# Two heads at once: scores as 64-row matmuls in an attention encoder on one Trainium2 core

## The chip, the cores and the metric

The kernel runs on one core of one Trainium2 chip. The metric is device time in microseconds (us) of one execution; lower is better. The core's engines work side by side and wait for one another through semaphores: TensorE (PE in the profile; PEld is its loading of stationary operands), VectorE (DVE), ScalarE (ACT), GpSimd (POOL) and SyncE (SP), which here only starts DMA transfers.

## What is computed

The reference is a two-layer encoder over 1024 tokens of width 1024, all in float32. Layer 0 uses mixer A (a neighbourhood attention), layer 1 uses mixer B (grouped-query attention). After each mixer come an output projection, a residual add and a gated per-layer embedding. The change touches mixer B, 16 query heads of width 64 that share 4 key/value heads:

```python
def mixer_b(h, w_in, q_norm_g, k_norm_g, w_out):
    proj = h @ w_in
    q, k, v, gate = jnp.split(proj, [MIX_WIDTH, MIX_WIDTH + kv_w, MIX_WIDTH + 2 * kv_w], axis=-1)
    q = rms_norm(q.reshape(b, s, B_Q_HEADS, HEAD_DIM), q_norm_g).transpose(0, 2, 1, 3)
    k = rms_norm(k.reshape(b, s, B_KV_HEADS, HEAD_DIM), k_norm_g).transpose(0, 2, 1, 3)
    ...
    q, k = _apply_axial_rope(q, tabs), _apply_axial_rope(k, tabs)
    ...
    sc = jnp.einsum('bkgqd,bksd->bkgqs', qb, k).astype(jnp.float32) * scale
    pr = jax.nn.softmax(sc, axis=-1).astype(v.dtype)
    o = jnp.einsum('bkgqs,bksd->bkgqd', pr, v)
    ...
    return (o * jax.nn.silu(gate)) @ w_out
```

## The kernel before, in words

**Number format.** TensorE takes fp32r operands, so a float32 value is held as a high part and a low part (names ending in h and l, or `KA` and `KB` for keys). A projection of two such operands is three matmuls: high by high, high by low, low by high (`split3`, all through the helper `mm`, line 300). That line therefore carries nearly all matmuls; they are told apart by the tiles they write: `d` a projection, `s` scores, `o` an attention output. `t` is written by transposes, which are TensorE instructions with a line of their own.

**Layout.** The normalised residual stream stands transposed in `HTh`/`HTl` and serves every projection. Weights come by DMA into `wstage` and are split into `wh`/`wl` by one ACT and one DVE instruction each (lines 215 and 216); a queue `WQ` brings them on in the order of use.

**One attention step of mixer B** covers one head and one tile of 128 queries, so there are 128 steps; they are listed with the two heads of a pair one after the other. A step has four parts:

- `f_S`: four matmuls write the scores of 128 queries by 1024 keys into `s` (two PSUM banks; there are two such buffers). The stationary tile `QS` has the head's query high part in the 64 partitions of one half and its low part in the other half; `KA` and `KB` hold the keys' high and low parts in both halves, so a matmul over 128 rows sums two products. Then DVE takes the row minimum `mn` (line 1047; the scores carry a minus sign).
- `f_E`: ACT computes the exponentials `P` and their row sums (line 1053).
- `f_T`: `P` is transposed in two blocks of four 128x128 transposes, each into a PSUM buffer `t` (two buffers). ACT writes the high part `PTh` (line 1065) and DVE the low part `PTl` (line 1066) out of each; after both the buffer is free.
- `f_AV`: on every second step, 16 matmuls multiply `V` by the `PTh` and `PTl` of two steps into `o`.

`q_stack` makes `QS`: four transposes of the rotated queries, a copy to `raw` on ACT, and for each head of the pair a cast of 64 rows on ACT (line 1029) and a subtraction on DVE (line 1030), the latter put off by two ticks. `head_end` takes a finished head out of `o` (an ACT copy, line 477, and a DVE sum, line 441, both on 64 rows), inverts the row sums and arranges gate, scaling and storing of a pair.

**What sets the order.** Each engine runs its instructions in the order in which the program lists them; nothing reorders them later. `mixer_b` lists 32 attention steps for each of four groups of heads, and `mix` lays the projection pieces of the group ("dense": gates, the next group's q, keys and values, and in the last group the products `pp`) between the parts of the steps, in the proportion of the weights that stand beside each part (`CB`, `CN`). After each part `pulse` moves the weight queue on by one and counts down work put off with `post.add(ticks, ...)`; `later` counts by steps. The order within the steps is

```python
att.append((later.tick, w[0]))
if av:
    att.append((lambda n=n: f_AV(*steps[n - 1]), w[1]))
te = [(lambda n=n: f_T(*steps[n]), w[2])]
if n + 1 < len(steps):
    te.append((lambda n=n: f_E(*steps[n + 1]), w[3]))
...
if n + 2 < len(steps):
    att.append((lambda n=n: f_S(*steps[n + 2]), w[4]))
```

so the scores run two steps ahead of the transposes and the exponentials one step. Before the groups a prologue projects the first keys, values and queries.

Of the kernel before, what the change touches and what calls it, by code (L numbers as in the profile page):

```python
# [21 lines left out]
NT = 8  # L22
# [8 lines left out]
CB = (1.25, 1.0, 2.0, 0.5, 1.0)  # L31
CN = (1.5, 0.0, 1.0, 1.0, 1.5)
# [5 lines left out]
FIN = (4, 4)  # L38
HOLD = 2
DP = 1  # L40
KD, KS = 3, 4
QD = (2, 5, 8)
QS_AT = 3
AGE, LAG = 3, 3
YS = (11, 11)
YLOAD_A, YLOAD_B = 1, 118
# [106 lines left out]
def trunk(ctx, tc, x, wts, rpb, gains, hgains, mask, rope, out):  # L153
# [275 lines left out]
    def head_end(sb, h, hf, rs, Ops, ylive, layer, gg, talloc):  # L429
        pair = h // 2  # L430
        b = (h % 2) * 64
        if h % 2 == 0:
            Y = sb.tile([128, 512], F32, name="Y", bufs=2)
            rb = sb.tile([128, 512], F32, name="rb", bufs=2)
            r8 = sb.tile([128, 8], F32, name="r8", bufs=4)
            ylive[pair, hf] = (Y, rb, r8, {})
        Y, rb, r8, tail = ylive[pair, hf]
        yh = Y[b:b + 64]

        def join():  # L440
            dve.scalar_tensor_tensor(yh, Ops[0:64], 0.5, yh, op0=ALU.mult, op1=ALU.add)

        def rows():
# [22 lines left out]
        def norm():  # L466
            dve.reciprocal(r8[:, 4 * (h % 2):4 * (h % 2) + 4], rs)
            if h % 2 == 0:
                return
# [6 lines left out]
        def evac():  # L476
            act.activation(yh, Ops[64:128], AF.Copy, scale=0.5)
            post.add(DY, join)
            norm()
        if h == NH - 1 and hf == 1:  # L480
            evac()
        else:
            post.add(DO[layer], evac)
        if h % 2 == 0:
            return None
        G = gg.pop((pair, hf))
        del ylive[pair, hf]

        def fin_last():
            dve.tensor_tensor(Y, Y, G, ALU.mult)  # L490
# [9 lines left out]
        def fin():  # L500
# [6 lines left out]
            def split():  # L507
                act.activation(yhi, Y, AF.Copy)  # L508
                dve.tensor_tensor(ylo, Y, yhi, ALU.subtract)
                post.add(2, lambda: (store(0, rb), store(1, Y)))  # L510
            pool.tensor_tensor(Y, Y, G, ALU.mult)
            pool.tensor_tensor(Y, Y, rb, ALU.mult)
            post.add(YS[layer], split)
        return fin_last if pair == 7 else fin

    def gate_items(key, pair, hf, alloc, sb, gg):
# [10 lines left out]
        return proj_T((key, pair), hf, alloc, evac, release=[(key, pair)] if hf else ())  # L527

    def pp_items(l, alloc, sb, tags):
        items = []  # L530
        for hf in range(2):
            for t in range(NT):
                def f(hf=hf, t=t):
                    ps = alloc()
                    wh, wl = WQ.get(("pp", l, hf))
                    for u in range(2):
                        ph, pl = WQ.get(("pt", l, u))
                        c = slice(u * 512, (u + 1) * 512)
# [769 lines left out]
```

## Time and profile before

| what | value |
|---|---|
| three timed runs | 1581.31, 1582.52, 1584.13 us; median 1582.52 us |
| the profiled execution's own time | 1586.45 us |
| its span, first to last instruction | 1584.7 us |
| PE busy | 1527.3 us (96%) |
| DVE busy | 1025.0 us (65%) |
| ACT busy | 872.8 us (55%) |
| POOL busy | 266.8 us (17%) |
| mixer B's attention groups | about 804 to 1389 us of the span |

The profile is of one execution. Busy time of an engine is the union of its instructions' times; a matmul's time includes the tail in which the next one already runs, so the distance between the starts of two matmuls is shorter than the time of one. Rows name a line, an engine, an operation, the tiles written and read, and the shape; "idle before" is how long the engine stood still just ahead of those instructions, and the name behind the arrow is what ended it. `d<-HTh,wh` reads: `d` is written, `HTh` is the moving operand and `wh` the stationary one.

### The profile page before, as it was taken

The page shows a single profiled execution, that of the slowest core. Times are in us where ns is not written, and L with a number is a line of the kernel's source. Part 1 is how long each engine was busy: PE and PEld are TensorE (multiplying, and loading weights), DVE is VectorE, ACT ScalarE, POOL GpSimd, SP SyncE. Part 2 cuts the span into 40 slices and gives each one's busy share as a digit, 9 for nine tenths or more (in the row PEclk, how much of TensorE's full clock was granted, in tenths as well). Part 3 has the DMA queues.
Part 4 walks back from the last instruction along what each step waited for, and adds up shares of the span by engine and source line. Part 5 has one row for each costly group of instructions (what it writes and reads, how often), then busy time and mean ns, then how long its engine had stood idle before and what let it go on. Part 6 is the DMA issues. An engine that isn't in the chain of part 4 may idle for free.

```text
span 1584.7 us, 24269 instructions
## 1 busy us (share of the span) xinstructions
PE 1527.3 (96%) x9048; PEld 1331.9 (84%) x9048; DVE 1025.0 (65%) x2062; ACT 872.8 (55%) x1744; POOL 266.8 (17%) x372
## 2 busy tenths in 40 slices
PE   6999999999999999999999999999999999999997
PEld 5888988988988788888888889989888888778886
DVE  6566576476477436558867776777776877625636
ACT  6465465466376522334467766667666777622422
POOL 2102102102112010000212222433131200000023
PEclk9999999999999999999999999999999999999999
DMA  8211122132123971232210111102111213651113
GB/s 270 77 47 63 58 73 77 39 92 77 39 88 91 335 244 59 76 137 78 71 48 21 38 59 43 48 24 68 36 33 41 74 34 103 237 199 54 68 56 130
DMA packets 89861, 138.84 MB, mean 88 GB/s; under 512 B 16912, under 2 KB 55952, under 8 KB 89744
## 3 DMA queue, kind: packets, MB, share of 16 engines
q1 hardware_dynamic: 85136, 122.62, 23.6%
q10 hardware_dynamic: 4608, 14.68, 2.6%
q8 instruction: 71, 1.16, 0.3%
q14 instruction: 46, 0.38, 0.1%
HBM read 104.65 MB, written 36.15 MB: 89 GB/s over the span
## 4 chain that ended last, share of the span: by engine, by line
PE 39%; DVE 6%; ACT 5%; issue 2%; POOL 0%; ACTq 0%; DVEq 0%
PE d L300 21%; PE o L300 6%; PE s L300 6%; PE t L1063 5%; DVE PTl L1066 2%; ACT PTh L1065 1%; ACT P L1053 1%; DVE mn L1047 1%; DVE QS L1030 1%; PE t L425 1%; ACT QS L1029 1%; ACT wh L215 0%; ACT rb L508 0%; DVE wl L216 0%; ACT th L1025 0%
## 5 line engine op out<-in xcount | busy, mean ns | idle before, releaser
L300 PE MATMUL d<-wh,HTh 128*128 128x256 f32 (+1 forms) x1096 | 373.0, 340 | 4.9 <-ACT HTh L426 2.3
L300 PE MATMUL d<-wh,HTl 128*128 128x256 f32 (+1 forms) x1096 | 366.5, 334 | 1.5 <-DVE HTl L427 1.5
L300 PE MATMUL d<-wl,HTh 128*128 128x256 f32 (+1 forms) x1096 | 365.9, 334 | 0.0
L300 PEld LDWEIGHTS d<-wh,HTh 128*128 128x128 f32 x1096 | 208.3, 190 | 28.3 <-ACT HTh L426 2.8
L300 PEld LDWEIGHTS d<-wh,HTl 128*128 128x128 f32 x1096 | 208.1, 190 | 23.9 <-DVE HTl L427 2.2
L1066 DVE TENSOR_TENSOR PTl<-t,PTh 128x512 fp32r<-128x512 f32 x256 | 164.6, 684 | 96.0 <-ACT PTh L1065 95.3
L300 PEld LDWEIGHTS d<-wl,HTh 128*128 128x128 f32 x1096 | 208.5, 190 | 21.5
L300 PE MATMUL d<-HTh,wh 128*128 128x512 f32 x504 | 206.2, 409 | 0.0
L300 PE MATMUL d<-HTh,wl 128*128 128x512 f32 x504 | 198.2, 393 | 0.0
L300 PE MATMUL d<-HTl,wh 128*128 128x512 f32 x504 | 197.9, 393 | 0.0
L300 PE MATMUL o<-PTl,V 128*128 128x256 f32 (+2 forms) x672 | 174.9, 291 | 2.9 <-DVE PTl L1066 2.5
L300 PE MATMUL o<-PTh,V 128*128 128x256 f32 (+2 forms) x672 | 173.9, 289 | 1.2 <-ACT PTh L669 1.1
L1053 ACT ACTIVATE P<-s,mn 128x1024 f32<-128x1024 f32 x128 | 142.5, 1113 | 54.2 <-DVE mn L1047 54.0
L1065 ACT ACTIVATE PTh<-t 128x512 fp32r<-128x512 f32 x256 | 140.1, 593 | 54.3 <-PE t L1063 53.9
L1047 DVE TENSOR_REDUCE mn<-s 128x1 f32<-128x1024 f32 x128 | 154.9, 1210 | 10.8 <-PE s L300 10.4
L1063 PE MATMUL t<-ident,P 128*128 128x128 f32 x1024 | 137.4, 275 | 7.9 <-DVE PTl L1066 7.0
L300 PE MATMUL s<-KA,QS 128*128 128x512 f32 (+2 forms) x384 | 134.7, 405 | 10.0 <-ACT PTh L1065 5.6
L216 DVE TENSOR_TENSOR wl<-wstage,wh 128x1024 fp32r<-128x1024 f32 x89 | 114.1, 1288 | 41.1 <-ACT wh L215 40.6
L300 PEld LDWEIGHTS o<-PTl,V 128*128 128x128 f32 x672 | 129.1, 192 | 9.1 <-DVE PTl L1066 4.8
L1063 PEld LDWEIGHTS t<-ident,P 128*128 128x128 f32 x1024 | 114.8, 140 | 23.8 <-DVE PTl L1066 18.6
L300 PEld LDWEIGHTS o<-PTh,V 128*128 128x128 f32 x672 | 128.7, 192 | 5.5 <-ACT PTh L669 1.3
L300 PE MATMUL s<-KB,QS 128*128 128x512 f32 (+2 forms) x384 | 122.3, 373 | 0.0
(178 smaller groups left out, 2440.7 us busy)
## 6 DMA issues: line engine op xcount, KB each, us to landing
wstage<-in_wts SPq DMA_DIRECT2D x92, 512.0 KB
X<-in_x SPq DMA_DIRECT2D x16, 512.0 KB
pp<-ppD SPq DMA_DIRECT2D x32, 256.0 KB
rb<-rD SPq DMA_DIRECT2D x56, 128.0 KB
ppD<-th SPq DMA_DIRECT2D x24, 256.0 KB
xD<-X SPq DMA_DIRECT2D x8, 512.0 KB
X<-xD SPq DMA_DIRECT2D x8, 512.0 KB
yD0h<-rb SPq DMA_DIRECT2D x14, 256.0 KB
```

The lines of the kernel that those rows point to most:

```text
L216: self.rest = lambda: dve.tensor_tensor(lo, s, hi, ALU.subtract)
L300: pe.matmul(ps, a, b, start=first, stop=last, skip_group_check=True)
L425: pe.transpose(ps[:, k], xn[:, (4 * c + k) * 128:(4 * c + k + 1) * 128], ident)
L1029: act.activation(qs[own], raw[own], AF.Copy)
L1030: post.add(DQ, lambda qs=qs, own=own, oth=oth: dve.tensor_tensor(qs[oth], raw[own], qs[own], ALU.subtract))
L1047: dve.tensor_reduce(mn, ps, axis=AX.X, op=ALU.min)
L1053: act.activation(p, ps, AF.Exp, bias=mn, scale=-1.0, accum_out=RS[h, hf][:, t:t + 1])
L1063: pe.transpose(ps[:, i], p[:, k * 128:(k + 1) * 128], ident)
L1065: act.activation(PTh[:, ks, c], ps, AF.Copy)
L1066: dve.tensor_tensor(PTl[:, ks, c], ps, PTh[:, ks, c], ALU.subtract)
```

## The change

One attention step now covers both heads of a pair and one tile of 128 queries, so there are 64 steps.

- `f_S` writes the scores of both heads, into both `s` buffers, with twelve matmuls over 64 rows: three products (query high by key high, query high by key low, query low by key high) times two halves of the keys times two heads. The heads alternate; one reads the upper 64 partitions of its operands, the other the lower 64. Two row minima follow.
- `q_stack` makes `QH` and `QL` for both heads with one ACT cast and one DVE subtraction on all 128 rows, straight from PSUM.
- `f_E` is called per head, `f_T` per head and block, so the four transposing blocks of a step are separate parts between which `mix` can lay projection pieces. `f_AV` follows in the same step and covers both heads.
- `f_S` runs one step ahead; all parts but the exponentials have the same weight (`CP`).
- The output is taken out of `o` on each second step, with ACT copies and DVE sums of 64 rows by 256 columns, twice as many as before; the pair's ending moves from `head_end` into `pair_end`, which mixer A uses too.
- Projection pieces are cut finer in the groups: gates into 8 pieces (4 before) for a half of the tokens, q and kv tiles into 4 (2 before), `pp` tiles into 2 (1 before). The y tiles that the next stage needs are loaded two to a step.

```diff
-CB = (1.25, 1.0, 2.0, 0.5, 1.0)
-CN = (1.5, 0.0, 1.0, 1.0, 1.5)
-FIN = (4, 4)
+FIN = (4, 2)
-QS_AT = 3
+QS_AT = 2
+CP = (0.0, 1.0, 1.0, 1.0, 1.0, 1.0, 1.0)
-YLOAD_A, YLOAD_B = 1, 118
+YLOAD_A, YLOAD_B = 1, 59
...
-                raw = sb.tile([128, 512], F32, name="th")
-                act.activation(raw, ps.rearrange("p t c -> p (t c)"), AF.Copy)
+                ps = ps.rearrange("p t c -> p (t c)")
+                qh, ql = [sb.tile([128, 512], F32R, name=n) for n in ("QH", "QL")]
+                act.activation(qh, ps, AF.Copy)
+                dve.tensor_tensor(ql, ps, qh, ALU.subtract)
+                QST[pair, hf] = qh, ql
...
-            steps = [(2 * p + j, hf, t) for p in range(8) for hf in range(2) for j in range(2) for t in range(4)]
+            steps = [(p, hf, t) for p in range(8) for hf in range(2) for t in range(4)]
...
+                ps = [psS.tile([128, 1024], F32, name="s") for _ in range(2)]
+                for i, (q, k) in enumerate(((qh, ka), (qh, kb), (ql, ka))):
+                    for c in (slice(0, 512), slice(512, 1024)):
+                        for j in range(2):
+                            o = slice(64 * j, 64 * j + 64)
+                            mm(ps[j][:, c], q[o, t * 128:(t + 1) * 128], k[o, c], i == 0, i == 2)
...
+                for n in range(16 * g, 16 * g + 16):
+                    att.append((later.tick, CP[0]))
+                    for i in range(4):
+                        att.append((lambda n=n, i=i: f_T(*steps[n], i // 2, i % 2), CP[1 + i]))
                     if n + 1 < len(steps):
-                        te.append((lambda n=n: f_E(*steps[n + 1]), w[3]))
...
+                        att.append((lambda n=n: f_S(*steps[n + 1]), CP[5]))
+                        for j in range(2):
+                            att.append((lambda n=n, j=j: f_E(*steps[n + 1], j), 0.0))
+                    att.append((lambda n=n: f_AV(*steps[n]), CP[6]))
...
-                    qi = q_items(g + 1, pool)
-                    kv = kv_items(1, pool) if g == 1 else [None, None]
+                    qi = q_items(g + 1, pool, 2)
+                    kv = kv_items(1, pool, 2) if g == 1 else [None, None]
...
-                    dense += gates(2 * g + 1) + pp_items(1, dalloc, sb, TAGS_B)
+                    dense += gates(2 * g + 1) + pp_items(1, dalloc, sb, TAGS_B, 2)
```

How the instructions stand on TensorE in the fourth group, before: two steps of one head, with gate pieces (`d`) of six matmuls.

```order
L1063 MATMUL t<-ident,P 128x128 x8
L300 MATMUL s<-KA,QS 128x512 x2
L300 MATMUL s<-KB,QS 128x512 x2
L300 MATMUL d<-HTh,wh_11989 128x512
L300 MATMUL d<-HTl,wh_11989 128x512
L300 MATMUL d<-HTh,wl_11990 128x512
L300 MATMUL d<-HTh,wh_11989 128x512
L300 MATMUL d<-HTl,wh_11989 128x512
L300 MATMUL d<-HTh,wl_11990 128x512
L1063 MATMUL t<-ident,P 128x128 x8
L300 MATMUL s<-KA,QS 128x512 x2
L300 MATMUL s<-KB,QS 128x512 x2
```

Both blocks of a step (x8) stand together, and a score and six projection matmuls part them from the next. After the change, one step of a pair in the same group:

```order
L1073 MATMUL t<-ident,P 128x128 x8
L299 MATMUL d<-HTh,wh_12136 128x512
L299 MATMUL d<-HTl,wh_12136 128x512
L299 MATMUL d<-HTh,wl_12137 128x512
L1073 MATMUL t<-ident,P 128x128 x4
L299 MATMUL d<-HTh,wh_12136 128x512
L299 MATMUL d<-HTl,wh_12136 128x512
L299 MATMUL d<-HTh,wl_12137 128x512
L1073 MATMUL t<-ident,P 128x128 x4
L299 MATMUL s<-KA,QH 128x512 x4
L299 MATMUL s<-KB,QH 128x512 x4
L299 MATMUL s<-KA,QL 128x512 x4
```

Four blocks of a pair now lie within one stretch, with pieces of three matmuls after the second and the third, and one run of twelve score matmuls follows.

On VectorE in that group, before, three steps' minima (`mn`), with a step's two low parts (`PTl` x2) between them:

```order
L1047 TENSOR_REDUCE mn<-s 128x1
L441 SCALAR_TENSOR_TENSOR Y<-o,Y 64x512
L1066 TENSOR_TENSOR PTl<-t,PTh 128x4x128 x2
L1047 TENSOR_REDUCE mn<-s 128x1
L509 TENSOR_TENSOR Y<-Y,rb 128x512
L1030 TENSOR_TENSOR QS<-th,QS 64x512 x2
L1066 TENSOR_TENSOR PTl<-t,PTh 128x4x128 x2
L1047 TENSOR_REDUCE mn<-s 128x1
```

and after:

```order
L1058 TENSOR_REDUCE mn<-s 128x1 x2
L1076 TENSOR_TENSOR PTl<-t,PTh 128x4x128
L513 TENSOR_TENSOR Y<-Y,rb 128x512
L1076 TENSOR_TENSOR PTl<-t,PTh 128x4x128
L1108 SCALAR_TENSOR_TENSOR Y<-o,Y 64x256 x2
L530 SCALAR_TENSOR_TENSOR G<-th,G 128x512
L1076 TENSOR_TENSOR PTl<-t,PTh 128x4x128 x2
L1058 TENSOR_REDUCE mn<-s 128x1 x2
```

The two minima of a pair stand together, ahead of all four low parts.

More of the change, by code (lines that the diff above doesn't have):

```diff
@@ L474, in norm @@
                 post.add(DT[hf], across)
[L476 to L487, printed above, removed]
         def fin_last():
+            G = gg.pop((pair, hf))
             dve.tensor_tensor(Y, Y, G, ALU.mult)
@@ L1125, in gates @@
                 def gates(p):
[L1126 removed]
+                    return [i for hf in range(2) for i in gate_items("bg", p, hf, dalloc, sb, gg, 1)]
                 dense = []
```

228 lines of the change are left out of this document (125 added, 103 removed).

## The prediction, made before the changed kernel was run

> **What bounds the kernel now.** I read first the windows, cut at the four groups of mixer B's attention (32 steps each, counted by their exponentials), with the prologue ahead. Columns: length, busy time of PE, PEld, DVE, ACT and POOL with instruction counts, PE clock, DMA share, GB/s.
>
> ```profile
> span 1584.7 us, 24269 instructions
> 737.00:804.00 67.00, 63.11 (x461) 59.47 (x460) 54.12 (x175) 29.53 (x73) 14.65 (x24) 0.97 0.21 66
> 804.00:933.00 129.00, 125.80 (x875) 112.05 (x874) 97.56 (x147) 95.09 (x174) 28.80 (x42) 1.00 0.11 31
> 933.00:1098.50 165.50, 161.57 (x1147) 148.75 (x1146) 119.68 (x212) 110.84 (x220) 58.90 (x112) 1.00 0.15 46
> 1098.50:1243.00 144.50, 137.07 (x942) 124.17 (x941) 105.47 (x169) 97.46 (x181) 32.83 (x48) 1.00 0.14 41
> 1243.00:1389.00 146.00, 140.07 (x856) 119.93 (x855) 106.93 (x159) 103.56 (x182) 11.33 (x12) 0.99 0.36 118
> ```
>
> PE is busy 95 to 98% of each group, DVE 72 to 76%, ACT 67 to 74%. So PE bounds, and the two others have a quarter in reserve. Second, the chain in order of time, in a stretch without stalls, gives what PE's work costs start to start:
>
> ```profile
> 1181.11 1.91 PE o L300 x16
> 1183.02 0.87 PE t L1063 x8
> 1183.89 0.93 PE s L300 x4
> 1184.82 1.39 PE d L300 x6
> ```
>
> A 512-column matmul takes 0.232 us, a 256-column one 0.119, a transpose 0.109. Now the groups' ideal: 32 x (0.87 + 0.93) + 16 x 1.91 = 88.2 us of attention in each; a group of q pieces (or kv) is 192 x 0.119 = 22.9, a gate pair 48 x 0.232 = 11.1, `pp` 96 x 0.232 = 22.3, four stackings 1.7. That makes 123.9, 158.8, 135.0 and 134.3, together 552 of the 585 us: 33 us are stalls. Third, the waits and rows that show of what kind these are (the first three from the wait list of mixer B's groups, the others from the timeline: start, length, engine, line, and in brackets the idle time before):
>
> ```profile
> PEld t L1063 <- DVE PTl L1066: 18.6, 40, 1.8
> DVE PTl L1066 <- ACT PTh L1065: 95.3, 67, 4.4
> ACT P L1053 <- DVE mn L1047: 48.2, 35, 4.1
> ...
> 1378.76 1.03 PE L1063 MATMUL t<-ident,P 128*128 128x128 f32 x8
> 1379.46 1.09 ACT L1065 ACTIVATE PTh<-t 128x512 fp32r<-128x512 f32 x2
> 1380.09 1.29 DVE L1066 TENSOR_TENSOR PTl<-t,PTh 128x512 fp32r<-128x512 f32 x2 [3.19 <-ACT PTh L1065]
> 1380.83 1.25 PE L1063 MATMUL t<-ident,P 128*128 128x128 f32 x8 [1.04 <-DVE PTl L1066]
> ```
>
> The last four are mixer B's last steps, where nothing is left to lay between two pairs of transposing blocks: the third block starts 1380.83 - 1378.76 = 2.07 us after the first, since it needs the buffer that ACT and then DVE must empty. In the bulk of the groups scores, projections and `o` lie there, and the wait is rare.
>
> **The change, part by part.**
>
> *Scores.* Before, two heads take 2 x 0.93 = 1.86 us. Now twelve 512-column matmuls over 64 rows. No row shows one, so the bounds are: the halves overlap, six slots, 6 x 0.232 = 1.39; or they follow one another, twelve slots, 2.79. I take 1.39: neighbours in the run read other partitions and write other `s` buffers, and loading is no bar, since twelve loads at the transposes' 0.109, each of which has its own, fit 1.31. Gain 0.46 a step, 64 steps: 29.7 us of PE work. [...]
>
> *Changing the array's shape.* Each run of twelve is entered from transposes over 128 rows and left again: 128 changes. No row has one. Lower bound 0: in the chain above scores follow transposes without a gap. Upper bound: the last matmul's tail plus a load that nothing hides:
>
> ```profile
> 1184.66 0.40 PE L300 MATMUL d<-HTh,wh 128*128 128x512 f32 x1
> 1184.90 0.39 PE L300 MATMUL d<-HTl,wh 128*128 128x512 f32 x1
> ```
>
> 0.40 - 0.232 = 0.16, plus 0.109: 0.27. Both ends are equally near, so the middle, 0.135. It counts at all 64 entries and at the exits where PE is then the late one (some 40): 104 x 0.135 = 14 us, bounds 0 and 28.
>
> *The order of the steps.* This is where gain is given back. Scores ran two steps ahead; now the next step's scores are issued after this step's last block, and four blocks of a pair must pass through two buffers. The rows for the links (group view, then timeline):
>
> ```profile
> L1066 DVE TENSOR_TENSOR PTl<-t,PTh 128x512 fp32r<-128x512 f32 x256 | 164.6, 684 | 96.0 <-ACT PTh L1065 95.3
> L1047 DVE TENSOR_REDUCE mn<-s 128x1 f32<-128x1024 f32 x128 | 154.9, 1210 | 10.8 <-PE s L300 10.4
> L1053 ACT ACTIVATE P<-s,mn 128x1024 f32<-128x1024 f32 x128 | 142.5, 1113 | 54.2 <-DVE mn L1047 54.0
> L1065 ACT ACTIVATE PTh<-t 128x512 fp32r<-128x512 f32 x256 | 140.1, 593 | 54.3 <-PE t L1063 53.9
> ...
> 879.97 0.62 PE L300 MATMUL s<-KB,QS 128*128 128x512 f32 x2
> 880.63 1.22 DVE L1047 TENSOR_REDUCE mn<-s 128x1 f32<-128x1024 f32 x1 [0.60 <-PE s L300]
> ...
> 1180.89 1.18 DVE L1047 TENSOR_REDUCE mn<-s 128x1 f32<-128x1024 f32 x1
> 1182.17 1.12 ACT L1053 ACTIVATE P<-s,mn 128x1024 f32<-128x1024 f32 x1 [1.52 <-DVE mn L1047]
> ```
>
> A minimum starts 0.04 after the scores' end, an exponential 0.10 after its minimum. From the start of a step's scores: 1.39 + 0.16 tail + 0.04 = 1.6; two minima to 4.0; the second head's exponential 4.1 to 5.2; only behind it on ACT `PTh` of the first block, to 5.8; `PTl` to 6.5; third block, a piece of 3 x 0.232 = 0.70, fourth block: 6.6 + 0.44 + 0.70 + 0.44 = 8.2 us until the next scores. PE's own work per step, from the ideals less 7.4 each, is 7.3, 9.5, 8.0 and 7.9. Where scores and `o` each have a piece behind them (third and fourth group), the first block starts at 1.39 + 0.70 + 1.91 + 0.70 = 4.7, and 4.7 + 2.07 + 1.58 = 8.4. On top come the queue's other instructions between `E` and the low parts: a stacking each fourth step (ACT 0.59, DVE 0.68 by the rows of that shape, in front of `PTh` and `PTl`), gates, weight splits, the outputs. I take 0.3 for the first group and 0.4 to 0.5 for the third and fourth (a stacking step costs about 1.1: its own 0.44 on PE, and 0.68 by which `PTl` of the first block comes later; outputs stand on ACT between the first two blocks' `PTh` and delay the fourth block by some 0.6). The second group has six pieces a step, one behind every block: first block to third is 2.3, over 2.07, so it stays PE-bound at 9.46 + 0.3. Groups: 16 x 8.5 = 136 (129.0 before), 16 x 9.76 = 156 (165.5), 16 x 8.9 = 142 (144.5), 16 x 8.8 + 5 for held pieces and the last step = 146 (146). Sum: +7 - 9.5 - 2 + 0 = -4.5 us. So of 29.7 some 25 go into waits on PE for `PTl` and `P`; behind the waiting third block stand in PE's queue a piece, the fourth block, the next scores and `o`, and with the scores everything on DVE and ACT.
>
> *Stacking.* Per pair and half ACT loses two casts, DVE one of two subtractions:
>
> ```profile
> L1030 DVE TENSOR_TENSOR QS<-th,QS 64x512 fp32r<-64x512 f32 x32 | 22.5, 704 | 1.5 <-ACT QS L1029 0.5
> L1029 ACT ACTIVATE QS<-th 64x512 fp32r<-64x512 f32 x32 | 20.2, 630 | 0.9
> 789.77 1.22 PE L300 MATMUL s<-KA,QS 128*128 128x512 f32 x2 [2.59 <-DVE QS L1030]
> ```
>
> 20 us of ACT and 11 of DVE go, off the path in the groups. On the path lies the prologue's wait, 2.59 us, and the slower clock behind it (0.97 of 67 us: 2 us). The new tiles are ready some 2 us sooner; I take -3 of the possible -4.6.
>
> *At nothing:* the output and the y loads.
>
> ```profile
> L477 ACT ACTIVATE Y<-o 64x512 f32<-64x512 f32 x64 | 38.0, 594 | 25.5 <-PE o L300 22.2 <-PE t L460 1.5 <-PE d L300 1.0
> L935 ACT ACTIVATE qt<-d 128x256 f32<-128x256 f32 x28 | 10.7, 384 | 19.8 <-PE d L300 19.6
> ACT th L543 <- DMA HTl<-yD1l: 3.7, 1, 3.7
> ```
>
> The output's ACT copies and DVE sums move the same elements in twice the instructions, beside PE, in the quarter that ACT and DVE have free; uncovered, two of 256 columns instead of one of 512 are 0.17 us more (2 x 0.384 - 0.594), 32 times 5.6 us. The 16 y loads on ACT's queue come two to a step instead of one to each of twice as many steps, so at the same rate; uncovered, one more wait of 3.7 us. Stores and row broadcasts on SP keep their ticks, which are as many per pair as before, and no transfer is added.
>
> *Sum.* 1586.45 (the profiled execution; span plus 1.75) - 4.5 - 3 + 14 = 1593; the median of the three runs is 3.9 lower, so 1589.
>
> **The rivals.**
>
> *Pieces cover the waits* (other side). If each engine's reserve swallows the links above, PE alone decides: -29.7 - 3, and all 128 changes at half my price, +9: 1559. For it: a quarter of DVE and ACT is free, and the 18.6 us row is small today. Against: 2.07 us is a latency, which reserve doesn't shorten. It decides where the third block's wait falls below 0.2 us a step.
>
> *The array empties at each change.* The upper price, 28 instead of 14: 1603. For it: no row denies it. Against: a matmul of another type follows a transpose today without gap. [...]
>
> *No overlap* (the change doesn't do what it says). Twelve slots: 64 x 1.39 = 89 more, 1678; with halves that overlap but loads that don't hide, about half of that, 1630. For it: no trace shows 64 rows. Against: nothing shared.
>
> **How the numbers follow.** My case (1575 to 1603, walk and shape change each uncertain by some 10 us): 0.44. Covered waits (1550 to 1575): 0.26. Emptying (1600 to 1612): 0.16. No or half overlap (1620 to 1680): 0.14. The range leaves out the last and the lowest eighth of the second, and takes in the top of the third: 1553 to 1616. A measurement here tells 0.2%, 3.2 us, from no change. Faster: 0.26 + 0.09 of my case below 1579.3 = 0.35; same: 0.12 of my case; slower: the rest, 0.53. My case alone spans both sides, likeliest just above today's time.
>
> **What would show it.** Right: twelve `s` matmuls start about 0.12 apart; `t` waits for `PTl` at a third block grow from 18.6 us to some 50; the first group gets longer, the second shorter. Wrong: starts 0.23 apart (no overlap); a hole of 0.2 us and more at both ends of each run (emptying); PE without waits at `t` and a shorter first group (covered).

## The result, and the profile after

| kernel | median | spread of the runs |
|---|---|---|
| before | 1582.06 us | 1581.31 to 1584.13 (4 runs) |
| after | 1659.92 us | 1657.5 to 1660.76 (4 runs) |

The ratio is 1.0487, 95% interval [1.0469, 1.0506]: the change costs 78 us. The two profiled executions, from which all views come, lie 71 us apart: 1586.45 us before, 1657.5 us after.

The page of after, its span and busy times:

```profile
span 1655.7 us, 24775 instructions
PE 1545.2 (93%) x9304; PEld 1305.5 (79%) x9304; DVE 1028.0 (62%) x2062; ACT 866.8 (52%) x1744; POOL 269.3 (16%) x372
```

PE's busy time grew by 18 us, that of the others hardly; the span grew by 71, and PE's share fell from 96% to 93%. So most of it is idle time. The windows of after, cut where the exponentials of each group begin and where the last one starts (columns as in the prediction):

```profile
793.00:947.40 154.40, 134.91 (x972) 111.90 (x971) 103.32 (x157) 94.90 (x176) 33.39 (x46) 0.99 0.10 30
947.40:1121.80 174.40, 163.28 (x1199) 140.98 (x1198) 116.66 (x211) 109.31 (x218) 57.59 (x109) 0.99 0.15 43
1121.80:1279.30 157.50, 142.42 (x1019) 118.75 (x1018) 106.55 (x171) 98.20 (x182) 33.92 (x49) 0.99 0.13 38
1279.30:1447.70 168.40, 139.54 (x856) 106.52 (x855) 102.86 (x149) 97.01 (x175) 12.19 (x14) 0.95 0.26 88
sum 654.70, PE 580.16 PEld 478.15 DVE 429.40 ACT 399.42 POOL 137.09; mean PE 145.04 PEld 119.54 DVE 107.35 ACT 99.85 POOL 34.27
```

Before, cut by the same marks, the groups took 137.2, 165.7, 144.5 and 134.0:

```profile
sum 581.40, PE 562.73 PEld 503.67 DVE 428.57 ACT 405.28 POOL 134.63; mean PE 140.68 PEld 125.92 DVE 107.14 ACT 101.32 POOL 33.66
```

The whole loss lies in the groups: 654.7 - 581.4 = 73 us. PE's idle time there went from 581.40 - 562.73 = 18.7 to 654.70 - 580.16 = 74.5 us, which is 56 of the 73. The other 17 are busy time; a lower clock (0.95 in the last group) makes up some 13 of them, as worked out below. What PE waited for, from the waits of weight loading in after's groups (total, times, longest):

```profile
PEld t L1073 <- DVE PTl L1076: 78.0, 82, 3.7
PEld d L299 <- issue: 17.8, 48, 0.5
PEld t L1073 <- DVE QL L1038: 16.3, 15, 1.9
PEld s L299 <- issue: 11.7, 46, 0.7
```

The transposes' wait for `PTl`, 18.6 us before, is 78.0. The wait for `QL`, which is the stacking's low part, is new. The rows with "issue" are loads that stand still without waiting for any engine that the profile names; many stand at the ends of the runs of 64 rows, and in the first experiment, without such runs, they are gone.

### The profile page after: what moved, and what is told of

It reads as the page before. It is cut to its first block, busy times and chain, and to the rows that moved or that the text cites. A ratio compares the mean times of both kernels' runs of the same rounds, so it can differ in the third digit from the quotient of the medians.

```text
span 1655.7 us, 24775 instructions
## 1 busy us (share of the span) xinstructions
PE 1545.2 (93%) x9304; PEld 1305.5 (79%) x9304; DVE 1028.0 (62%) x2062; ACT 866.8 (52%) x1744; POOL 269.3 (16%) x372
## 5 line engine op out<-in xcount | busy, mean ns | idle before, releaser
L299 PE MATMUL d<-wh,HTh 128*128 128x256 f32 (+1 forms) x1096 | 381.0, 348 | 5.2 <-ACT HTh L425 1.7
L1076 DVE TENSOR_TENSOR PTl<-t,PTh 128x512 fp32r<-128x512 f32 x256 | 172.9, 688 | 136.3 <-ACT PTh L1075 135.0
L1073 PE MATMUL t<-ident,P 128*128 128x128 f32 x1024 | 159.3, 283 | 68.7 <-DVE PTl L1076 53.3
L299 PE MATMUL d<-HTh,wh 128*128 128x512 f32 x504 | 212.4, 421 | 2.1 <-ACT G L525 2.1
L1075 ACT ACTIVATE PTh<-t 128x512 fp32r<-128x512 f32 x256 | 149.5, 595 | 84.1 <-PE t L1073 82.5
L1058 DVE TENSOR_REDUCE mn<-s 128x1 f32<-128x1024 f32 x128 | 150.7, 1219 | 39.0 <-PE s L299 38.5
L681 DVE TENSOR_TENSOR PTl<-t,PTh 128x384 fp32r<-128x384 f32 (+1 forms) x128 | 66.6, 521 | 77.8 <-ACT PTh L680 76.8
L299 PEld LDWEIGHTS d<-HTh,wl 128*128 128x128 f32 x504 | 94.7, 188 | 21.6
```

The source lines that it names most:

```text
L299: pe.matmul(ps, a, b, start=first, stop=last, skip_group_check=True)
L681: dve.tensor_tensor(PTl[:, sl], ps[:, :m], PTh[:, sl], ALU.subtract)
L1058: dve.tensor_reduce(mn, ps[j], axis=AX.X, op=ALU.min)
L1073: pe.transpose(ps[:, i], e[:, k * 128:(k + 1) * 128], ident)
L1075: act.activation(PTh[:, ks, c], ps, AF.Copy)
L1076: dve.tensor_tensor(PTl[:, ks, c], ps, PTh[:, ks, c], ALU.subtract)
```

## Did the halves overlap?

The timeline of after, TensorE, around one score run in the third group (start, length, engine, line, form, count):

```profile
1179.94 0.60 PE L1073 MATMUL t<-ident,P 128*128 128x128 f32 x4
1180.47 0.73 PE L299 MATMUL s<-KA,QH 64*128 64x512 f32 x4
1181.05 0.62 PE L299 MATMUL s<-KB,QH 64*128 64x512 f32 x4
1181.50 0.63 PE L299 MATMUL s<-KA,QL 64*128 64x512 f32 x4
1182.07 0.39 PE L299 MATMUL d<-wh,HTh 128*128 128x256 f32 x1
1182.29 0.28 PE L299 MATMUL d<-wl,HTh 128*128 128x256 f32 x1
1182.41 0.27 PE L299 MATMUL d<-wh,HTl 128*128 128x256 f32 x1
...
1190.05 0.73 PE L299 MATMUL s<-KA,QH 64*128 64x512 f32 x4
```

Yes. Four matmuls take 1181.50 - 1181.05 = 0.45 us where four of 128 rows took 0.93; the two halves start together (within 0.01 us), and pairs follow each other about 0.23 us apart. The first four take 0.58 and the last four 0.57, each 0.12 to 0.13 more than the middle: I put that down to the change of shape, going in and coming out. It also shows outside the run. The four transposes ahead take 0.53 up to the run, 0.09 more than 4 x 0.109, and the first matmul behind it takes 1182.29 - 1182.07 = 0.22 to the next one, 0.10 more than those that follow. So the run of twelve itself takes 1.60 us, but costs TensorE 1.60 + 0.09 + 0.10 = 1.79, against 1.86. By the starts, 58 of the 64 runs in after, those at full clock, show the same (0.09 ahead, 1.59, 0.11 behind). The gain for TensorE is about 0.07 a step, some 4 us in 64 steps. The price of both changes is 1.79 - 1.39 = 0.40 a step, 26 us where I took 14 (bounds 0 and 28). So a delay of about 0.2 us stands at either end of the run; no row shows what the array does there.

The next run starts 1190.05 - 1180.47 = 9.58 us later. PE's own work in a step of this group, as I had it, is 8.0 us. So the run got shorter as meant, and the step around it got longer.

## The experiments

**Theory.** The order of the steps set the loss: scores, two minima, two exponentials, then `PTh` and `PTl` form a chain on DVE and ACT that ends later than PE's work, and every other instruction that stands in those two queues between its links lengthens it. **Rivals.** The 64-row matmuls and their shape changes are what costs; the finer pieces cost; the paired y loads cost. Ratios below are to before, with 95% intervals; the median of before was between 1582 and 1584 us throughout.

**1. After's order without the 64-row run.** Each head's scores by four matmuls of 128 rows on stacked `QS`, as before. The making of `QS` goes back with them (a copy first, casts of 64 rows, the subtraction put off); everything else is as after.

```diff
-                for i, (q, k) in enumerate(((qh, ka), (qh, kb), (ql, ka))):
-                    for c in (slice(0, 512), slice(512, 1024)):
-                        for j in range(2):
+                for j in range(2):
+                    for i, k in enumerate((ka, kb)):
+                        for c in (slice(0, 512), slice(512, 1024)):
...
+                            mm(ps[j][:, c], QST[p, hf, j][:, t * 128:(t + 1) * 128], k[:, c], i == 0, i == 1)
```

> The changed kernel's order of steps, with the scores as before: eight matmuls over 128 rows per pair (QS made as before), instead of twelve over 64. Theory order (the new order lets the transposing blocks wait for their buffers, the 64-row run itself gains: 12 start within 1.60 us against 2 x 0.93): 1665 to 1690 us, slower than the changed kernel by up to 0.26 x 64 = 17. Theory array (the 64-row run and its changes of shape cost what was lost): within 10 us of 1582.

Measured: 1676.16 us, 1.0585 [1.057, 1.0601]. The loss stays without a single 64-row matmul and is 16 us larger. The waits of weight loading in its groups:

```profile
PEld t L1074 <- DVE PTl L1077: 95.9, 87, 3.5
```

So the 64-row matmuls do not make the loss, and that rival falls. The 16 us are what the overlap takes off, together with whatever the other making of the queries costs; run 16 puts back one part of that, the copy, and it costs 2 us in this order.

**2. The y tiles one to a step**, from step 56 on, instead of two to a step from 59 on.

```diff
-                    if YLOAD_B <= n < YLOAD_B + NT // 2:
-                        for t in (2 * (n - YLOAD_B), 2 * (n - YLOAD_B) + 1):
-                            att.append((lambda t=t: load_y(1, t), 0.0))
+                    if YLOAD_B <= n < YLOAD_B + NT:
+                        att.append((lambda t=n - YLOAD_B: load_y(1, t), 0.0))
```

> The changed kernel with the y tiles loaded one to a step from step 56 on, instead of two to a step from step 59 on. Theory order with the loads as an own part of the last group's loss (ACT stands 2 us for issuing in one step after 1408 us): 1648 to 1655. Rival, loads hidden: 1660 within 3.

Measured: 1654.22 us, 1.0448 [1.0432, 1.0463], 5.7 us less than after. The timeline of after shows how two loads in one step stand in ACT's queue (ACTq), between the exponentials and the copies:

```profile
1409.26 1.88 ACTq L263 DMA_DIRECT2D HTh<-yD1h  x1
1411.74 0.77 ACT L1112 ACTIVATE Y<-o 64x256 f32<-64x256 f32 x2 [2.02 <-issue]
1412.55 0.85 DVE L1108 SCALAR_TENSOR_TENSOR Y<-o,Y 64x256 f32<-64x256 f32 x2 [4.04 <-ACT Y L1112]
1414.17 1.12 PE L1073 MATMUL t<-ident,P 128*128 128x128 f32 x4 [3.00 <-DVE PTl L1076]
```

Issuing one of these transfers held ACT for 1.88 us; the output copy, then DVE, then the transposes on PE came late behind it.

**3. Pieces in two places only**, behind the second block and behind `o`, to give the third block its cover in one lump.

```diff
-CP = (0.0, 1.0, 1.0, 1.0, 1.0, 1.0, 1.0)
+CP = (0.0, 0.0, 2.0, 0.0, 0.0, 0.0, 2.0)
```

> The changed kernel with weights that put a step's projection pieces at two places alone, half behind the second transposing block and half behind o. First block to third is then 0.87 + 1.4 = 2.27 us of PE work, over the 2.07 that ACT and DVE need for a buffer. Theory order: 1600 to 1635. Theory array: 1660 within 5. Rival, ACT and DVE are late because of their queues and not because PE comes early: 1645 to 1665.

Measured: 1679.12 us, 1.0599 [1.0579, 1.062]. The waits of weight loading in its groups:

```profile
PEld t L1073 <- DVE PTl L1076: 47.6, 51, 2.8
PEld d L299 <- ACT qt L946: 16.6, 17, 1.4
PEld d L299 <- ACT G L525: 15.3, 10, 2.5
PEld d L299 <- ACT th L554: 10.8, 5, 3.6
```

A miss. The wait for `PTl` fell by 30 us, and projections now wait 43 us for ACT in these three rows, 7 in after: there is one projection buffer `d`, and two tiles cannot follow each other until ACT has emptied it. A second limit, which the prediction did not have.

**4. One link of the chain made longer.** The second head's minimum is computed twice; 64 x about 1.2 us more on DVE and nothing on PE.

```diff
                     dve.tensor_reduce(mn, ps[j], axis=AX.X, op=ALU.min)
+                    if j:
+                        dve.tensor_reduce(mn, ps[j], axis=AX.X, op=ALU.min)
```

> The changed kernel with the second head's row minimum taken twice: 1.2 us more on DVE between the scores and that head's exponential, 64 times 77 us of DVE. Theory order with the chain scores, two minima, exponential, low parts, third block as what sets the step: 50 to 75 us slower, 1710 to 1735. Theory array (PE sets the step): 1660 to 1672.

Measured: 1734.5 us, 1.0957 [1.0938, 1.0975], 75 us more than after: about as much as the added DVE time, although DVE was busy only 62% of the span. Its groups, cut by the same marks:

```profile
sum 730.30, PE 604.26 PEld 497.59 DVE 506.10 ACT 401.38 POOL 136.27; mean PE 151.07 PEld 124.40 DVE 126.52 ACT 100.35 POOL 34.07
```

DVE has 506.10 - 429.40 = 77 us more, and PE's idle time is 730.30 - 604.26 = 126.0 us, 51.5 more than in after. So two thirds came through as waits. The rest is PE's busy time, in which the slower clock has a part: 82 us of the groups ran at half clock, 27 in after (the mean granted clock of the whole span was 0.975 against 0.99). It is also uneven, 28, 14, 11 and 23 us in the four groups, where 19 were added to each, so that the sum is so near the whole is partly luck. Still, DVE's time at this place of the step is on the path in all four groups. This is the sharpest evidence for the chain.

**5. Scores earlier.** The next step's scores go between the second and the third block, the two minima behind the fourth low part; pieces laid to suit, y tiles as in 2.

```diff
-CP = (0.0, 1.0, 1.0, 1.0, 1.0, 1.0, 1.0)
+CP = (0.0, 1.0, 0.0, 0.0, 1.0, 1.0, 1.0)
...
+                        if i == 1 and n + 1 < len(steps):
+                            att.append((lambda n=n: f_S(*steps[n + 1]), CP[5]))
                     if n + 1 < len(steps):
-                        att.append((lambda n=n: f_S(*steps[n + 1]), CP[5]))
+                        att.append((lambda n=n: f_M(*steps[n + 1]), 0.0))
```

> The changed kernel with its 64-row scores, but in another order: the next step's scores stand between a step's second and third transposing block (both exponentials they need to free the s buffers are done by then), the two row minima are issued behind the fourth block's low part, pieces follow the first block, the scores, the fourth block and o; y tiles one to a step. First block to third is then at least 0.87 + 1.6 us of PE work, and minima and exponentials have the fourth block, pieces and o to hide behind. Theory order: waits of t for PTl fall from 78 us to under 25 and the time to 1565 to 1595. Theory array: 1654 within 5, as with the y loads alone.

Measured: 1660.98 us, 1.048 [1.0458, 1.0501]; nothing gained, and 7 us more than run 2, which has the same y loads. The waits of weight loading in its groups:

```profile
PEld t L1077 <- ACT P L1068: 36.8, 48, 1.6
PEld o L299 <- DVE PTl L1080: 27.7, 56, 3.1
PEld t L1077 <- DVE PTl L1080: 11.9, 15, 2.1
```

A miss: the wait for `PTl` at `t` went as meant, from 78 to 12 us. Most of it came back, 30 us as a wait for the exponentials, since both minima now stood behind the last low part and the exponentials behind both, and 28 us as a wait of `o` for the last `PTl`.

**6. The same with 128-row scores** (the edit of 1 on top of 5).

```diff
+                for j in range(2):
+                    for i, k in enumerate((ka, kb)):
...
```

> The order of e5_early with the scores over 128 rows, eight matmuls per pair. Theory order, 64-row run worth 0.26 us a step where PE is the bound: 10 to 17 us slower than e5_early. Theory array (the 64-row run gains nothing once PE is the bound): equal to it within 3.

Measured: 1676.1 us, 1.0582 [1.056, 1.0601], 15 us more than 5, as much again as between run 1 and after, and again with the old making of the queries in it.

**7. As 5, pieces only behind the fourth block, the scores and `o`.**

```diff
-CP = (0.0, 1.0, 0.0, 0.0, 1.0, 1.0, 1.0)
+CP = (0.0, 0.0, 0.0, 0.0, 1.0, 1.0, 1.0)
```

> As e5_early, but no pieces behind the first block, so that pieces lie behind the scores, the fourth block and o alone. Theory order: first block to third is covered all the same, within 8 us of e5_early; if the one projection buffer d is a second limit, which evacuations on ACT hold, it is slower by 5 to 20 since pieces stand closer together.

Measured: 1687.71 us, 1.0647 [1.0628, 1.0666]. Fewer places for pieces cost 27 us over 5, with the waits of 3 (`d` for `qt` 14.2 us, for `G` 12.7). The one `d` buffer again.

**8. After with the pieces as coarse as before.**

```diff
-                    qi = q_items(g + 1, pool, 2)
+                    qi = q_items(g + 1, pool)
...
-                    dense += gates(2 * g + 1) + pp_items(1, dalloc, sb, TAGS_B, 2)
+                    dense += gates(2 * g + 1) + pp_items(1, dalloc, sb, TAGS_B)
```

> The changed kernel with the projection pieces as coarse as before (gates in 4, q and kv tiles in 2, pp tiles in 1), its order of steps otherwise. Theory order: half as many places with a piece, more third blocks that follow the first within 2.07 us, 1665 to 1700. Rival, the finer pieces themselves cost: 1640 to 1655.

Measured: 1676.1 us, 1.0575 [1.0559, 1.0592], 16 us more than after. The finer pieces help; that rival falls.

**9. The two minima parted.** As 5, but the first head's minimum stands right behind the scores, ahead of the third and fourth low parts, and only the second's behind them.

```diff
-                            att.append((lambda n=n: f_S(*steps[n + 1]), CP[5]))
+                            att.append((lambda n=n: (f_S(*steps[n + 1]), f_M(*steps[n + 1], 0)), CP[5]))
...
-                        att.append((lambda n=n: f_M(*steps[n + 1]), 0.0))
+                        att.append((lambda n=n: f_M(*steps[n + 1], 1), 0.0))
```

> As e5_early, but the first head's row minimum is issued right behind the scores and ahead of the third and fourth block's low parts, the second head's behind them. In e5_early DVE stands idle for 2 us between the second and third low part while both minima are queued behind the fourth. Theory order (what is lost is the time in which a step's DVE and ACT work waits in its queue for something that comes later): the waits of t for P fall from 37 us to under 12 and the time to 1595 to 1630. Rival (DVE and ACT have too much to do in a step, wherever it stands): 1650 to 1665.

Measured: 1627.66 us, 1.0282 [1.0265, 1.0299]. Moving 64 instructions of 1.2 us by two places in DVE's queue gives 33 us back: the same instructions on every engine, another order on one. The waits of weight loading:

```profile
PEld o L299 <- DVE PTl L1079: 42.7, 59, 3.2
PEld t L1076 <- DVE QL L1038: 11.3, 13, 2.3
PEld t L1076 <- ACT P L1067: 3.3, 6, 0.8
```

The wait for the exponentials is gone (36.8 to 3.3), part of it is back at `o`, which waits for the last `PTl`.

**10. As 9, with half a piece moved from the first to the fourth block.**

```diff
-CP = (0.0, 1.0, 0.0, 0.0, 1.0, 1.0, 1.0)
+CP = (0.0, 0.5, 0.0, 0.0, 1.5, 1.0, 1.0)
```

> As e9_split_minima, with half of the pieces behind the first block moved behind the fourth, so that o comes later after the last low part. Theory order: the waits of o for PTl fall by some 10 us, 1590 to 1630. Rival (the projection buffer d): slower than e9_split_minima by 5 to 15, since pieces stand closer together.

Measured: 1626.22 us, 1.0276 [1.026, 1.0291]. The wait at `o` fell from 42.7 to 26.6 us, and the waits at `t` took 9 of these 16 (for `QL` 11.3 to 15.5, for `PTl` 9.2 to 13.9). No gain that could be told.

**11. As 10, `o`'s eight high matmuls ahead of its eight low ones, and the stacking of the queries moved up behind the scores.**

```diff
                 for k in range(NT):
-                    mm(o, v, PTh[:, k], t % 2 == 0 and k == 0, False)
-                    mm(o, v, PTl[:, k], False, t % 2 == 1 and k == NT - 1)
+                    mm(o, V[p // 2][:, k], PTh[:, k], t % 2 == 0 and k == 0, False)
+                for k in range(NT):
+                    mm(o, V[p // 2][:, k], PTl[:, k], False, t % 2 == 1 and k == NT - 1)
```

> As e10_split_minima_late, and the attention output runs its eight high parts before its eight low parts (0.95 us more until the first PTl is needed), and the stacking of the next queries stands behind the scores, not in front of the first transposing block. Theory order: the waits of o for PTl (27 us) and of t for QL (15 us) fall to a third, 1590 to 1612. Rival (DVE and ACT have too much to do wherever it stands): 1620 to 1630.

Measured: 1627.04 us, 1.0272 [1.0257, 1.0288]. The wait at `o` fell to 3.3 us, the one for `QL` rose from 15.5 to this:

```profile
PEld t L1076 <- DVE QL L1038: 29.9, 15, 2.8
```

Two edits with opposite signs; 13 undoes the second.

**12. The order of 11 with 128-row scores.**

```diff
+                for j in range(2):
+                    for i, k in enumerate((ka, kb)):
...
```

> The order of e11_high_first with the scores over 128 rows. If PE is the bound there, the difference is the full price of a step's scores with their two changes of shape: by the starts in the changed kernel's trace (1.60 against 1.86 us) 17 us slower. If the changes of shape cost more than the run's own length shows (weight loads stand 31 us), the difference falls below 10.

Measured: 1634.87 us, 1.0321 [1.0304, 1.0339], 7.8 us over 11. The second expectation was the right one: the changes of shape cost more than the run's own length shows, 0.09 us ahead of it and 0.10 behind. But the edit also puts the old making of the queries back, and with it goes the wait for `QL`, 29.9 us in 11, so that 8 us are not the price of the overlap alone. One reading fits the three orders and is not shown: where the chain sets the step, it sees the run's own length, 1.60 against 1.86 us, which is 17 us in 64 steps (16 and 15 measured); where PE sets it, PE sees 1.79 against 1.86.

**13. As 11 with the stacking left behind `o`.**

```diff
-                            m = n + QS_AT
-                            if m % 4 == 0 and m < len(steps):
-                                pn, fn, _ = steps[m]
-                                att.append((lambda pn=pn, fn=fn: q_stack(pn, fn), 0.0))
```

> The second early order (the run before last but one: one minimum right behind the scores, the other behind the low parts, pieces moved by one link), with the output's eight high matmuls ahead of its eight low ones, and the stacking of the queries left behind the outputs where it was. Theory order: the outputs' wait for PTl (26.6 us there) falls to about 3, the transposes' wait for QL stays at about 15 and does not grow to 30 as it did when the stacking was moved up, so 1626 - 15 to 20 = 1607 to 1613. Rival (a wait that is removed comes back at the next link whatever is done): 1622 to 1628.

Measured: 1616.65 us, 1.0211 [1.019, 1.0233], 9.6 us less than 10, between the two expectations. `o` waits 6.6 us, `t` for `QL` 19.8. Of 20 us taken away at `o` half came through.

**14. As 13, with the stacking's transposes in the projection buffer `d`,** asked for four steps ahead instead of two.

```diff
-                return pd.tile([128, 512], F32, name="d")
+                if not pro[0]:
+                    while due:
+                        q_stack(*due.pop(0), pd.tile([128, 512], F32, name="d").rearrange("p (t c) -> p t c", t=4))
+                return pd.tile([128, 512], F32, name="d")
```

> The same as the run before it in this set, but 15 of 16 stackings of the queries put their transposes into a projection buffer, at the ends of tiles, asked for four steps ahead, so that the transposes of the probabilities no longer stand behind them. Theory order: the transposes' wait for QL (about 15 us) falls under 5 and 5 to 12 us come back: 1597 to 1608. Rival (the single projection buffer is the next limit): matmuls of d wait for the queries' copies instead, 10 us or more, and the time is within 4 us of the run before it. Rival (changes of shape cost the rest): the time can not fall below before's 1582 plus about 31 for the idle loads, so 1613 or above for both.

Measured: 1643.22 us, 1.0373 [1.0355, 1.039], 27 us worse than 13. The waits of weight loading:

```profile
PEld d L299 <- DVE QL L1047: 39.9, 15, 4.8
```

The second expectation had the cause, not the size: a stacking holds the single `d` up to 4.8 us, longer than any wait for `QL` at one of the two `t` in 13 (2.6). The slower clock came with it: 41 us of the groups ran at half clock, none in 13 (the mean granted clock of the whole span was 0.986 against 0.999).

**15. As 13, with one part of the change undone in the stacking:** its transposes are copied out first, by one ACT instruction as before, and `QH` and `QL` are made from the copy.

```diff
-                act.activation(qh, ps, AF.Copy)
-                dve.tensor_tensor(ql, ps, qh, ALU.subtract)
+                raw = sb.tile([128, 512], F32, name="th")
+                act.activation(raw, ps.rearrange("p t c -> p (t c)"), AF.Copy)
+                act.activation(qh, raw, AF.Copy)
+                dve.tensor_tensor(ql, raw, qh, ALU.subtract)
```

> The rearranged order with the output's high matmuls first (the best so far), and of the change one thing undone: the stacking's transposes are first copied out by one ACT instruction, as before, and QH and QL are made from that copy, so that the transposing buffer is free after the copy and not only after QL. Theory order (each wait gives its time back): the transposes' wait for QL (19.8 us there) is gone, a wait for the copy of at most 5 us takes its place, and the time falls by 10 to 15: 1601 to 1607. Rival (the 0.6 us more of ACT per stacking lie on the path, in front of the same PTh): within 4 us of 1616.6, the wait only renamed.

Measured: 1608.53 us, 1.0153 [1.0136, 1.0171], 8 us less than 13 and the least of all rearranged orders. The waits of weight loading, and its groups cut by the same marks:

```profile
PEld t L1077 <- DVE PTl L1080: 15.9, 21, 2.2
PEld t L1077 <- ACT th L1036: 9.7, 11, 1.9
PEld o L299 <- DVE PTl L1080: 6.8, 15, 1.1
...
sum 602.20, PE 563.94 PEld 478.30 DVE 424.53 ACT 404.01 POOL 140.74; mean PE 140.99 PEld 119.58 DVE 106.13 ACT 101.00 POOL 35.19
```

19.8 us of waits for `QL` became 9.7 us for the copy (`th`): the transposing buffer is free one DVE instruction sooner. PE is idle 602.20 - 563.94 = 38.3 us, and busy as long as in the kernel before.

**16. The kernel after with that copy alone.**

```diff
-                act.activation(qh, ps, AF.Copy)
+                act.activation(raw, ps.rearrange("p t c -> p (t c)"), AF.Copy)
+                act.activation(qh, raw, AF.Copy)
...
```

> The kernel after, with that same one thing undone: a copy of the stacking's transposes first, QH and QL from the copy. Theory order: here the four blocks behind the stacking wait for PTl and for the exponentials anyway, so part of the 16.3 us of waits for QL only moves: 5 to 15 us back, 1645 to 1655, and the wait for PTl grows by what is not given back. Rival (the copy lies on the path): 1656 to 1664.

Measured: 1661.83 us, 1.0494 [1.0475, 1.0513]; no gain, against the theory's 5 to 15. The wait of 16.3 us for `QL` became 5.8 for the copy, and the wait for `PTl` took it all:

```profile
PEld t L1074 <- DVE PTl L1077: 89.6, 87, 4.1
```

That says when a removed wait pays. In after the step is one closed chain of DVE and ACT, and a wait taken out of PE's queue comes back at the next link. In 15 PE is more often the late one (38.3 us of idle time in the groups against 74.5), and 8 of 10 us come through.

## Why the prediction was wrong, by its own steps

**The scores** were right: they overlap, six slots of 0.23 us. **Changing the array's shape** was mis-sized: 26 us instead of 14, just within its bounds, because the delay also stands in the matmuls around the run. That leaves TensorE 4 us of the 29.7. **The prologue** was right: the wait for `QS` is gone and the first exponential starts at 793.0 instead of 795.6. A small slip in the sums: the terms listed for the second group add to 157.9 us, not 158.8; it moves the forecast by less than 1 us.

**The order of the steps** is the step that failed, and there the size of one term. Its walk was right where nothing else stands in the queues. In the first group scores started at 875.52; the rows on DVE and ACT until the third block:

```profile
877.22 2.35 DVE L1058 TENSOR_REDUCE mn<-s 128x1 f32<-128x1024 f32 x2 [0.84 <-PE s L299]
879.67 1.12 ACT L1064 ACTIVATE P<-s,mn 128x1024 f32<-128x1024 f32 x1
880.77 1.07 ACT L1075 ACTIVATE PTh<-t 128x512 fp32r<-128x512 f32 x2
881.40 1.29 DVE L1076 TENSOR_TENSOR PTl<-t,PTh 128x512 fp32r<-128x512 f32 x2 [1.82 <-ACT PTh L1075]
```

Minima from 1.70, the second exponential at 4.15, `PTh` at 5.25, `PTl` at 5.88, each about 0.1 from the forecast; the next scores started 8.5 us after those of 875.52. But I added 0.3 to 0.5 us a step for "the queue's other instructions between `E` and the low parts". The groups took 154.4, 174.4, 157.5 and 168.4 us. That is 9.65 a step in the first (9.45 without its first step, in which the end of the prologue lies), 10.9 and 9.8 in the next two, and 11.1 in the fourth, whose window holds 15 steps, instead of 8.5, 9.76, 8.9 and 8.8. Over the walk without extras (8.2, 9.46, 8.4 and 8.4) it is 1.3 to 2.7 us a step. The changes of shape are 0.4 of it and the slower clock 0.1 to 0.6; some 0.7 to 1.8 are left for the extras, where I took 0.3 to 0.5. My estimate from these figures: of the 64 us by which the forecast missed, roughly two thirds are the extras, and the rest are the changes of shape and the clock. By the starts of their score runs, the four steps of the third and fourth group that hold almost nothing else took 8.8 us (1171.7, 1208.9, 1247.7 and 1334.7), those with a stacking alone 9.4 to 10.0, and the two with a pair of weight splits 12.7 and 13.2, part of that at the slower clock. Stacking and outputs had a price in my list; gates and weight splits stood there without one. One place in the fourth group, whose step took 13.2 us (ACT, then DVE, then TensorE):

```profile
1293.98 1.12 ACT L1064 ACTIVATE P<-s,mn 128x1024 f32<-128x1024 f32 x1
1295.08 2.00 ACT L214 ACTIVATE wh<-wstage 128x1024 fp32r<-128x1024 f32 x2
1296.98 1.07 ACT L1075 ACTIVATE PTh<-t 128x512 fp32r<-128x512 f32 x2
...
1296.16 3.04 DVE L215 TENSOR_TENSOR wl<-wstage,wh 128x1024 fp32r<-128x1024 f32 x2 [2.28 <-ACT wh L214]
1299.12 1.27 DVE L1076 TENSOR_TENSOR PTl<-t,PTh 128x512 fp32r<-128x512 f32 x2
...
1299.85 1.25 PE L1073 MATMUL t<-ident,P 128*128 128x128 f32 x8 [3.27 <-DVE PTl L1076]
```

Two weight splits stood between the exponential and `PTh` on ACT (2.00 us) and ahead of `PTl` on DVE (3.04), and PE stood for 3.27 us. Before, the scores ran two steps ahead, and all such queues together left PE idle for 18.7 us in the groups; that the lead is the reason is argued, since no run changed the lead alone. In after every instruction of that kind lies in the loop itself, and run 4 measured that what is added there comes through, two thirds of it as PE's idle time alone. I had the chain and treated its load as a remainder.

**What hung on it.** I forecast that the `t` waits would grow from 18.6 to some 50 us; they grew to 78. The second group was forecast to stay bound by PE and shorter by 9.5 us; it got 9 longer.

**The slower clock** was in no term. After's groups hold eight stretches of 3.41 us each with a granted clock of 0.50. Two of them, each with the 3.41 us ahead of it (columns as above, the clock third from the end):

```profile
898.67:902.08 3.41, 1.35 (x11) 0.99 (x10) 1.63 (x3) 2.55 (x6) 0.00 (x0) 1.00 0.32 118
902.08:905.49 3.41, 3.41 (x18) 3.41 (x18) 1.18 (x2) 1.46 (x3) 0.00 (x0) 0.50 0.02 5
1298.03:1301.44 3.41, 1.59 (x11) 1.30 (x11) 2.37 (x4) 0.57 (x3) 0.00 (x0) 1.00 0.57 189
1301.44:1304.85 3.41, 3.41 (x15) 1.91 (x13) 1.29 (x2) 0.53 (x2) 0.00 (x0) 0.50 0.34 121
```

The second pair lies at the hole just shown; the first follows a hole of only 1.69 us. The eight starts lie whole multiples of 3.41 us apart. Cut into slices of that length, after's groups show what went ahead: in the slice before each slow one PE was idle for 1.82 to 2.91 us, in no other for more than 1.71, and no single hole in the groups was longer than 3.27. In before the border is less sharp: it has one slow stretch just ahead of the groups, after a slice with 2.25 us of idle time, and one just behind them, after 1.37, while slices in its groups with up to 1.4 were followed by none. By the mean clocks of the groups (0.95 of 168 us, 0.99 of the other three) this costs at most some 13 us of the 73; before had no such stretch in its groups.

**At nothing:** the y loads were not at nothing. Run 2 gives 5.7 us; I had a wait of 3.7 as the uncovered price, and "the same rate" was the wrong measure, since it is the place of two loads in one step that holds ACT (1.88 us for one issue in after's timeline). The **stacking** "off the path in the groups" was wrong in the open orders (8 us, run 15), hidden by the chain in after (run 16).

**The rivals.** "Pieces cover the waits" fell by its own mark: 78 / 64 = 1.2 us a step at the transposes, not under 0.2. "The array empties at each change" came nearly true in its price, at 26 us of its 28 and with 0.2 us at both ends of a run, the sign that I gave for it; but no row shows that the array empties, and the rival forecast 1603 and cannot make 78. "No overlap" would have given a time near the one measured, 1630 to 1678, and is refuted: its mechanism does not occur. A time that fits is not a cause.

**What stays open.** Run 15 is still 25 us over before. Within the groups it is 602.2 - 581.4 = 21 us, and PE's idle time there is 38.3 - 18.7 = 20 us more, so it is waits. PE's busy time is no smaller, because the score runs save it nothing in that order: by the starts, 62 runs take 0.11 ahead, 1.64 and 0.11 behind, 1.85 us together, against 1.86 before. Not tested alone were the output in twice as many instructions, which I had at nothing, and how far ahead the scores run: one pair fills both `s` buffers. A version faster than both kernels was not found.

## What to carry to other kernels

When a change takes steps together, walk the new chain through the queues of the engines that are not the bottleneck, with every instruction that stands there in a real step; the share of busy time did not show it here, and in the closed chain of after added time on an engine that is idle a third of the span came through almost whole (run 4: 77 us more on DVE, 75 us more in all, 51.5 of them as PE's idle time). To see whether a chain is closed, lengthen one link: if most of it shows in the time, look for an order that opens it before removing single waits. The place of one reduction was worth more here (33 us, run 9) than the whole gain in matmuls (29.7 forecast, some 4 found).

## What the runs showed of the hardware that I had not expected

- Matmuls over 64 rows on the two halves run at once: four of them in 0.45 us, where four over 128 rows take 0.93.
- Going into and out of such a run cost 0.12 us each at its first and last four matmuls, 0.09 ahead of it and 0.10 in the first matmul behind it, 0.40 in all; weight loads stood idle there by about 0.25 to 0.37 us each (11.7 us in 46, 17.8 in 48) without any wait that the profile names.
- In after's groups eight stretches of 3.41 us ran at half clock, each after a hole on PE of 1.7 to 3.3 us, and in the 3.41 us before each PE was idle for 1.82 to 2.91 us; in before one such stretch came after 1.37 us of idle time, and none after the slices in its groups with up to 1.4. My estimate from the clock of 0.50: such a stretch costs up to half of its 3.41 us, 1.7, if PE has work all through it.
